# Scaling the probability rows before the turn, one norm chain for two latents, and a step less for the last heads

## The chip, the cores and the metric

The kernel runs on one core of one Trainium2 chip. The metric is the time of one execution on the device, in microseconds (us); lower is better. The engines are named as the profile names them: PE (TensorE, the matrix engine; PEld is its weight load), DVE (VectorE), ACT (ScalarE), POOL (GpSimd) and SP (SyncE, which here only issues transfers). PSUM is the memory that PE writes to, SBUF the working memory; a PSUM bank holds 128 x 512 values of float32.

## The reference, cut to what matters

The program computes two blocks over 256 tokens of width 1024. The first (a mixer and a mixture of experts) is not touched by the change. The second has two layers; each is a mixer, a norm, a convolved feed-forward part and a gate. The first layer's mixer (`mixer_ab`) holds two attentions with eight heads each, the second's (`mixer_c`) a differential attention:

```python
def mixer_ab(x, ...):
    h = x @ w_in
    qa, ka = rope(h[..., :o1]), rope(h[..., o1:o2]); va = h[..., o2:o3]
    out_a = dilated_mixture(qa, ka, va)              # 8 heads of 64
    cq = rms_norm_2(h[..., o3:o4], q_norm, RMS_EPS)  # latent of 384
    ckv = rms_norm_2(h[..., o4:o5], kv_norm, RMS_EPS)  # latent of 256
    qb, kv = cq @ w_q_up, ckv @ w_kv_up
    ...
    out_b = dense_attention(qb, kb, vb, (B_NOPE + B_ROPE) ** -0.5)  # softmax(q k) v, 8 heads
    return concatenate([out_a, out_b]) @ w_out

def mixer_c(x, ...):
    a = softmax(q k / 8)                             # two maps a head, 8 heads
    o = (a[:, :, 0] - lam * a[:, :, 1]) @ v
    return (rms_norm_2(o, subln, LN_EPS) * (1.0 - lambda_init)) @ w_out
```

The dilated mixture of three windows is computed by the kernel as one softmax over all 256 keys, with the logarithm of how often a key is counted added to the scores.

## The kernel before, in words

Everything is in SBUF as 128 partitions by columns; 256 tokens are two halves m = 0, 1. Large matmuls run in three passes with operands split into a high and a low part: ACT copies the high part (`xH`, `w`, `abH`), DVE subtracts it from the source for the low part (`split`, line 463). Weights stream in order: `stream` loads them ahead and splits some pieces ahead of their use (`w<-raw` on ACT, `w<-raw,w` on DVE), each time that `take` asks for the next piece.

The order on every engine is that of the program; nothing is reordered later, and each engine takes its instructions in order. Inside the program, two attentions are written as generators, and a planner (`Side`, line 383) decides where their steps are placed between the projections' matmuls. `Clocked` (line 341) keeps an estimated clock for PE, ACT and DVE: each instruction adds a cost from its columns (DVE: 0.07 us + columns / 960; PE with plain float32: columns / 600) and 0.13 us where it reads what another instruction wrote, that of its own engine too unless both are PE's. A step is due when the last ACT or DVE result of the step before is ready, plus 0.15. After each block of projection matmuls, `side.tick` asks whether the estimated PE clock has reached the due time of the next step, and if so writes the step there, one at most. Of two neighbouring jobs, the one with the earlier due time goes first. `side.finish` writes the remaining steps of a job one after another. All instructions of these engines are recorded under one line (L379), so groups are told apart by tiles.

In `mixer_ab` the latents (`lat`, 672 columns: 384, 256 and 32) come from projection `ab_c`. For each of two latents ACT squares and sums both halves (`j`, `ss`), and DVE runs a chain: one instruction for the mean, ten for the inverse root (`rsqrt`, line 471: a start and three Newton steps of three), and two that scale `lat`. Then the rotation of the last 32 columns, and projection `ab_a` (`tokens(0)`), whose weight halves DVE splits in the same queue.

`pair_attention` (line 1969) serves both attentions with two heads a pair, four pairs p: `turn_head` of the pair before, `score_pair`, `soft` (row maximum on DVE, exponential `pe` with row sum `sm` on ACT), `weigh` of the pair two back (matmuls with the values, then `split` to `abH`, `abL`), a yield, and `diagonal` for both heads; another yield. `diagonal` puts the inverse row sums on a diagonal: two products of the identity, 128 x 128 each. `turn_head` multiplies `pe` by that diagonal, four matmuls a head, which turns the probabilities (keys to the partitions) and scales them at once, and ACT copies the bank to `pp`. `attention_a` is the dilated one (tiles `qkT`, `lnc`, `va`), `attention_b` the one over latents (`bT`, `vb`).

In `mixer_c`, `attention(n, src)` handles two heads, n = 0 to 3: turn q and k; a yield; scores and `soft` of both maps; a yield; the inverse sums, lam, and four DVE products that combine the two maps in `pe`; a yield; `turn_head` without a diagonal, by transposes; a yield; the weighted sum (`oc`), its norm on DVE; a yield; the turn to `ycH` (ACT) and `ycL` (DVE). The output projection `c_out` (`lin_sq`, line 1453) takes its four quarters in order. Quarter 0 is four blocks of six matmuls; quarters 1 to 3 have two blocks each for the first token half, then the second half follows. Quarter 3 reads the result of n = 3.

Of the kernel before, what the change touches and what calls it, by code (L numbers as in the profile page):

```python
# [13 lines left out]
OP = mybir.AluOpType  # L14
# [405 lines left out]
def program(ctx, tc, A, out, dump=None):  # L420
# [11 lines left out]
    def T(shape, name, dt=F32, tag=None):  # L432
        n = 4
        for s in shape[1:]:
            n *= s
        if tag is None:
            for t, lim in (("us", 128), ("uh", 512), ("u1", 1024), ("u2", 2048), ("u4", 4096), ("u8", 8192)):
                if n <= lim:
                    tag = t
                    break  # L440
        uid[0] += 1
        t = sb.tile(list(shape), dt, tag=tag, bufs=BUFS.get(tag, 1), name=f"{name}{uid[0]}")
        return t
# [1485 lines left out]
        for m in range(2):  # L1929
            S.activation(e[:, m], p2[:, m], AF.Exp, bias=nb[:, m:m + 1], scale=scale, accum_out=sm[:, m:m + 1])  # L1930

    def diagonal(r):

        n = r.shape[1]
        d = T([128, n, 128], "diag", tag="u1")
        V.reciprocal(r, r)
        for m in range(n):
            V.tensor_scalar(d[:, m], ident, r[:, m:m + 1], None, op0=OP.mult)
        return d

    def score_pair(get, p, add=None):

# [11 lines left out]
                add(ps)  # L1954
        return banks

    def turn_head(t, e, d=None):

        ps = PS()
        for m in range(2):  # L1960
            for k in range(2):
                o, i = ps[:, (k * 2 + m) * 128:(k * 2 + m) * 128 + 128], e[:, m, k * 128:k * 128 + 128]
                if d is None:
                    P.transpose(o, i, ident)
                else:
                    P.matmul(o, i, d[:, m], start=True, stop=True)
        S.activation(t, ps.rearrange("p (k t) -> p k t", k=2), AF.Copy)

    def pair_attention(get, scale, add, v, y, base, ready=lambda: True):

        probs, pts = {}, {}
        yH, yL = y

        def weigh(p):

            ps, pt = PS(), pts.pop(p)
            for k in range(2):
                for a in range(2):
                    c = slice(p * 128 + a * 64, p * 128 + a * 64 + 64)
                    P.matmul(ps[a * 64:a * 64 + 64, :256], v[:, k, c], pt[:, a, k], start=k == 0, stop=k == 1)  # L1980
            split(yH[:, base + p], yL[:, base + p], ps[:, :256])

        for p in range(6):
            while p > 1 and not ready():
                yield 0.5
            if 0 < p < 5:
                pts[p - 1] = T([128, 2, 2, 256], "pp")
                for a in range(2):
                    turn_head(pts[p - 1][:, a], *probs.pop(2 * p - 2 + a))
            if p < 4:  # L1990
                banks = score_pair(get, p, add)
            if p < 4:
                new = []
                for ps in banks:
                    e, s = T([128, 2, 256], "pe"), T([128, 2, 2], "sm")
                    soft(ps, scale, e, s[:, 0], s[:, 1])
                    new.append((e, s[:, 1]))
            if p > 1:
                weigh(p - 2)
            if p < 4:  # L2000
                yield
                for a, (e, sm) in enumerate(new):
                    probs[2 * p + a] = e, diagonal(sm)
            yield

    def ple_proj(i, p):
# [13 lines left out]
    def mixer_ab(x, evac):  # L2020
# [20 lines left out]
            lin_tok("ab_c", 2 * n, 2, xs, range(2), 336, lambda m, ps: S.activation(lat[:, m, n * 336:n * 336 + 336], ps[:, :336], AF.Copy),  # L2041
                    hold=0 if n else 4, ready=None if n else ready)
        dump("x2", x)
        for c0, w, g in ((0, 384, "ab_q_g"), (384, 256, "ab_kv_g")):
            ss = T([128, 2], "ss3")
            for m in range(2):
                j = T([128, 384], "j3")
                S.activation(j[:, :w], lat[:, m, c0:c0 + w], AF.Square, accum_out=ss[:, m:m + 1])
            V.tensor_scalar(ss, ss, 1 / w, 1e-6, op0=OP.mult, op1=OP.add)
            r = rsqrt(ss, 2)  # L2050
            for m in range(2):
                V.scalar_tensor_tensor(lat[:, m, c0:c0 + w], lat[:, m, c0:c0 + w], r[:, m:m + 1], Rc(g), op0=OP.mult, op1=OP.mult)
        for m in range(2):
            rope2(lat[:, m, 640:].unsqueeze(1), "b", m, 1)
        qk = [T([128, 2, 512], "qa"), T([128, 2, 512], "ka")]
# [87 lines left out]
    def mixer_c(x, evac):  # L2143
        xf = T2([128, 8, 256], "x")
        xs = xs_of(xf)
        yH, yL = T2([128, 8, 256], "yc")

        there = {}

        def attention(n, src):  # L2150


            def get(j):
                h, q = j // 2, slice((j % 2) * 64, (j % 2) * 64 + 64)
                return qk[0][q, h], qk[1][q, h], qk[0][q, 2 + h], qk[1][q, 2 + h]

            qk = to_feat(src, 4)
            yield
            nb, sm = (lambda t: (t[:, 0], t[:, 1]))(T([128, 2, 2, 2, 2], "sm"))
            banks = [ps for h in range(2) for ps in score_pair(get, h)]  # L2160
            es = (lambda t: (t[:, 0], t[:, 1]))(T([128, 2, 2, 2, 256], "pe"))
            for j, ps in enumerate(banks):
                a, h = j % 2, j // 2
                soft(ps, 0.125, es[h][:, a], nb[:, a, h], sm[:, a, h])
            yield
            V.reciprocal(sm[:, 1], sm[:, 1])
            V.scalar_tensor_tensor(sm[:, 1], sm[:, 1], lam, sm[:, 0], op0=OP.mult, op1=OP.mult)
            for h, e in enumerate(es):
                for m in range(2):
                    V.scalar_tensor_tensor(e[:, 0, m], e[:, 1, m], sm[:, 1, h, m:m + 1], e[:, 0, m], op0=OP.mult, op1=OP.add)  # L2170
            sq = T([128, 2, 2], "s2")
            V.scalar_tensor_tensor(sq, sm[:, 0], 1e-5, sm[:, 0], op0=OP.mult, op1=OP.mult)
            yield
            pts = T([128, 2, 2, 256], "pp")
            for h, e in enumerate(es):
                turn_head(pts[:, h], e[:, 0])
            yield
            while n not in there:
                yield 0.5
            ps, vc = PS("oc"), there.pop(n)  # L2180
            for h in range(2):
                for m in range(2):
                    c = slice((2 * m + h) * 128, (2 * m + h) * 128 + 128)
                    for k in range(2):
                        P.matmul(ps[:, c], pts[:, h, k, m * 128:m * 128 + 128], vc[:, k, h * 128:h * 128 + 128], start=k == 0, stop=k == 1)
            o, o2 = (T([128, 4, 128], w) for w in ("oc", "oc2"))
            S.activation(o.rearrange("p h d -> p (h d)"), ps, AF.Copy)
            S.activation(o2.rearrange("p h d -> p (h d)"), ps, AF.Square)
            v = T([128, 4], "cv")
            V.tensor_reduce(v, o2, axis=AX, op=OP.add)  # L2190
            v2 = v.rearrange("p (m h) -> p m h", m=2)
            V.scalar_tensor_tensor(v2, v2, 1 / 128, sq.rearrange("p h m -> p m h"), op0=OP.mult, op1=OP.add)
            r = rsqrt(v, 4)
            V.tensor_tensor(o, o, r.unsqueeze(2).to_broadcast([128, 4, 128]), op=OP.mult)
            yield
            ps = PS()
            for h in range(2):
                for m in range(2):
                    P.transpose(ps[:, h * 256 + m * 128:h * 256 + m * 128 + 128], o[:, 2 * m + h], ident)
            k, p2 = slice(2 * n, 2 * n + 2), ps.rearrange("p (a t) -> p a t", a=2)  # L2200
            S.activation(yH[:, k], p2, AF.Copy, scale=sg)
            V.scalar_tensor_tensor(yL[:, k], p2, sg, yH[:, k], op0=OP.mult, op1=OP.subtract)

        jobs = []

        def ready(m):
            feat_tile(xf, x, m, 8)

        for w, n in C_ORDER:
            if w:  # L2210
                vc = T([128, 2, 256], "vc")
                lin_tok("c_v", n, 1, xs, range(2), 256, lambda m, ps: S.activation(vc[:, m], ps[:, :256], AF.Copy))
                there[n] = vc
                if n == 1:
                    load_p(1)
                continue
            qk = T([128, 2, 512], "qk")
            lin_tok("c_qk", 2 * n, 2, xs, range(2), 512, lambda m, ps: S.activation(qk[:, m], ps, AF.Copy),
                    hold=0 if n else 4, ready=None if n else ready)
            for m in range(2):  # L2220
                rope2(qk[:, m].rearrange("p (h d) -> p h d", d=64)[:, :, :16], "a", m, 8)
            if n > 1:
                side.finish(jobs[n - 2])
            jobs.append(side.add(attention(n, qk), jobs[-1] if jobs else None))
        split_p()
        lin_sq("c_out", xs_of((yH, yL)), evac, {q: lambda q=q: side.finish(jobs[q]) for q in range(4)})
        dump("ycH", yH)
# [136 lines left out]
```

## Time and profile before

| What | us |
|---|---|
| Median of 3 runs | 1422.9 |
| Lowest and highest run | 1419.89, 1423.99 |
| The profiled execution | 1417.77 |
| Its span, first to last instruction | 1416.0 |
| PE busy in it | 1365.2 |
| DVE busy | 836.7 |
| ACT busy | 635.8 |

Times in the profile count from the first instruction of the span. A busy time is the sum over an engine's instructions; the ends of matmuls are modelled, since they are pipelined, so the distance between starts says more than the length of one. The first mixer takes some 700 to 842 us, the second some 1080 to 1180 us. [...]

### The profile page before, as it was taken

Reading aid. Unit: us, or ns where it says so; the run is one execution under the profiler, and the core shown is the slowest. Engines: PE = TensorE matmul, PEld = TensorE weight load, DVE = VectorE, ACT = ScalarE, POOL = GpSimd, SP = SyncE. Lnnn points to the kernel's source line nnn. Section 1 sums busy time; section 2 is a strip of 40 time slices with the busy share of each in tenths; the row PEclk is TensorE's granted clock in tenths of the full one; section 3 lists DMA queues with packets and bytes.
Section 4 is the critical chain, followed back from the end, with each engine's and each line's share of the span. In section 5 each row is a group of like instructions: output and inputs, shape, how many; then the busy total and the mean of one; then the engine's idle time right before and its main releaser. Section 6 shows DMA issues by size and latency. Waiting matters only on the chain.

```text
span 1416.0 us, 20480 instructions
## 1 busy us (share of the span) xinstructions
PE 1365.2 (96%) x8334; PEld 1064.8 (75%) x8334; DVE 836.7 (59%) x1517; ACT 635.8 (45%) x1021; POOL 8.3 (1%) x15
## 2 busy tenths in 40 slices
PE   5999999999999899999999899999999998999998
PEld 2678899878797444343488679999978887999996
DVE  4777457445866511211475586666676888566675
ACT  4643465534433311111356555445536664455541
POOL 0000000000000000000000000000000000000000
PEclk9999999999999999999999999999999999999999
DMA  9523334635469799999742345655544354555630
GB/s 370 223 71 119 149 150 153 250 125 190 175 212 360 301 421 421 421 421 421 283 179 90 120 149 181 207 179 208 175 156 146 127 179 139 188 179 180 216 140 30
DMA packets 44482, 297.42 MB, mean 210 GB/s; under 512 B 5171, under 2 KB 6371, under 8 KB 10017
## 3 DMA queue, kind: packets, MB, share of 16 engines
q1 hardware_dynamic: 41868, 291.02, 54.6%
q10 hardware_dynamic: 1924, 3.27, 0.7%
q0 software_dynamic: 592, 1.79, 0.5%
q8 instruction: 67, 1.10, 0.3%
q14 instruction: 31, 0.25, 0.0%
HBM read 295.00 MB, written 1.05 MB: 209 GB/s over the span
## 4 chain that ended last, share of the span: by engine, by line
PE 58%; DVE 5%; ACT 2%; issue 1%; DVEq 0%; ACTq 0%
PE ps L379 48%; PE pd L379 7%; DVE w L379 1%; PE pa L379 1%; PE pq L379 1%; ACT pe L379 1%; DVE v L379 1%; PE oc L379 1%; DVE sm L379 1%; DVE rs L379 0%; ACT w L379 0%; DVE xL L379 0%; DVE rsa L379 0%; ACT xH L379 0%; ACT oc L379 0%
## 5 line engine op out<-in xcount | busy, mean ns | idle before, releaser
L379 DVE TENSOR_TENSOR w<-raw,w 128x1024 fp32r<-128x1024 f32 (+3 forms) x301 | 346.5, 1195 | 84.6 <-ACT w L379 83.5
L379 ACT ACTIVATE w<-raw 128x1024 fp32r<-128x1024 f32 (+3 forms) x301 | 293.5, 1033 | 10.8 <-DVE w L379 4.8
L379 PE MATMUL ps<-xH,w 128*128 128x256 f32 x1408 | 256.5, 283 | 0.6 <-ACT xH L379 0.6
L379 PEld LDWEIGHTS ps<-xH,w 128*128 128x128 f32 x1408 | 220.6, 192 | 1.8 <-ACT xH L379 1.1
L379 PE MATMUL ps<-xL,w 128*128 128x256 f32 x704 | 199.4, 283 | 0.7 <-DVE xL L379 0.7
L379 PE MATMUL ps<-w,xH 128*128 128x512 f32 (+2 forms) x544 | 150.3, 362 | 4.0 <-ACT xH L379 2.1
L379 PEld LDWEIGHTS ps<-xL,w 128*128 128x128 f32 x704 | 135.0, 192 | 1.8 <-DVE xL L379 1.1
L379 PE MATMUL pd<-w,fh 128*128 128x512 f32 x528 | 125.6, 395 | 0.0
L379 PE MATMUL ps<-raw,xg 128*64 128x512 f32 x512 | 120.0, 600 | 0.0
L379 PE MATMUL ps<-hH,w 128*128 128x256 f32 (+1 forms) x608 | 115.7, 287 | 0.0
L379 PEld LDWEIGHTS pd<-w,fh 128*128 128x128 f32 x528 | 98.2, 189 | 21.6
L379 PEld LDWEIGHTS ps<-w,xH 128*128 128x128 f32 x544 | 95.4, 189 | 19.3 <-ACT xH L379 4.0
L379 PEld LDWEIGHTS ps<-hH,w 128*128 128x128 f32 (+1 forms) x608 | 94.9, 187 | 7.9 <-issue 2.7
L379 PE MATMUL ps<-w,xL 128*128 128x512 f32 (+2 forms) x272 | 97.8, 360 | 1.9 <-DVE xL L379 1.7
L379 PE MATMUL ps<-w,hH 128*128 128x512 f32 (+1 forms) x288 | 88.1, 390 | 0.0
L379 PE MATMUL ps<-hL,w 128*128 128x256 f32 (+1 forms) x304 | 85.9, 283 | 0.0
L379 PEld LDWEIGHTS ps<-raw,xg 128*64 128x64 f32 x512 | 33.3, 137 | 55.7 <-issue 51.9
L379 DVE SCALAR_TENSOR_TENSOR fc<-ps,par,fc 128x255 f32<-128x255 f32 x88 | 42.4, 482 | 51.5 <-ACT fc L379 49.9
L379 ACT ACTIVATE fc<-ps,par 128x256 f32<-128x256 f32 x44 | 24.8, 564 | 92.3 <-PE ps L379 66.4
L379 PEld LDWEIGHTS ps<-w,hH 128*128 128x128 f32 x288 | 52.2, 188 | 13.8 <-issue 2.7
L379 PEld LDWEIGHTS ps<-w,xL 128*128 128x128 f32 x272 | 51.3, 189 | 11.9 <-DVE xL L379 5.1
L379 PE MATMUL ps<-raw,hid 128*64 128x512 f32 x256 | 57.4, 593 | 0.0
(445 smaller groups left out, 1858.7 us busy)
## 6 DMA issues: line engine op xcount, KB each, us to landing
raw<-in_moe_gu SPq DMA_DIRECT2D x63, 1024.0 KB, 14.1
raw<-in_moe_down SPq DMA_DIRECT2D x32, 1024.0 KB, 12.8
raw<-in_mod SPq DMA_DIRECT2D x24, 1024.0 KB, 5.0
raw<-in_ffn_gate SPq DMA_DIRECT2D x22, 1024.0 KB, 4.8
raw<-in_ffn_up SPq DMA_DIRECT2D x22, 1024.0 KB, 4.9
raw<-in_ffn_down SPq DMA_DIRECT2D x22, 1024.0 KB, 4.8
raw<-in_w_brg SPq DMA_DIRECT2D x12, 1024.0 KB, 5.9
raw<-in_ple_gate SPq DMA_DIRECT2D x8, 1024.0 KB, 4.8
```

Source lines behind the costliest of these rows:

```text
L379: return f(*args, **kw)
```

## The change

Four edits. (1) In `mixer_ab`, `diagonal` is replaced by `scaled`: DVE multiplies the probability rows by the inverse row sums in place, and `turn_head` turns them by transposes in both mixers. (2) `weigh` no longer calls `split`: both parts are written by DVE, the high part by a copy, the low part by the subtraction. (3) The two latents' sums go into one tile, and one `rsqrt` over four columns serves both. (4) In `mixer_c`, the yield between `soft` and the combination of the two maps falls away for n = 3.

```diff
-    def diagonal(r):
-
-        n = r.shape[1]
-        d = T([128, n, 128], "diag", tag="u1")
+    def scaled(e, r):
+
         V.reciprocal(r, r)
-        for m in range(n):
-            V.tensor_scalar(d[:, m], ident, r[:, m:m + 1], None, op0=OP.mult)
-        return d
+        for m in range(2):
+            V.tensor_scalar(e[:, m], e[:, m], r[:, m:m + 1], None, op0=OP.mult)
+        return e
...
-    def turn_head(t, e, d=None):
+    def turn_head(t, e):
 
         ps = PS()
         for m in range(2):
             for k in range(2):
-                o, i = ps[:, (k * 2 + m) * 128:(k * 2 + m) * 128 + 128], e[:, m, k * 128:k * 128 + 128]
-                if d is None:
-                    P.transpose(o, i, ident)
-                else:
-                    P.matmul(o, i, d[:, m], start=True, stop=True)
+                P.transpose(ps[:, (k * 2 + m) * 128:(k * 2 + m) * 128 + 128], e[:, m, k * 128:k * 128 + 128], ident)
...
-            split(yH[:, base + p], yL[:, base + p], ps[:, :256])
+            V.tensor_copy(yH[:, base + p], ps[:, :256])
+            V.tensor_tensor(yL[:, base + p], ps[:, :256], yH[:, base + p], op=OP.subtract)
...
-                    turn_head(pts[p - 1][:, a], *probs.pop(2 * p - 2 + a))
+                    turn_head(pts[p - 1][:, a], probs.pop(2 * p - 2 + a))
...
-                    probs[2 * p + a] = e, diagonal(sm)
+                    probs[2 * p + a] = scaled(e, sm)
...
-        for c0, w, g in ((0, 384, "ab_q_g"), (384, 256, "ab_kv_g")):
-            ss = T([128, 2], "ss3")
+        latents = ((0, 384, "ab_q_g"), (384, 256, "ab_kv_g"))
+        ss = T([128, 2, 2], "ss3")
+        for i, (c0, w, _) in enumerate(latents):
             for m in range(2):
                 j = T([128, 384], "j3")
-                S.activation(j[:, :w], lat[:, m, c0:c0 + w], AF.Square, accum_out=ss[:, m:m + 1])
-            V.tensor_scalar(ss, ss, 1 / w, 1e-6, op0=OP.mult, op1=OP.add)
-            r = rsqrt(ss, 2)
+                S.activation(j[:, :w], lat[:, m, c0:c0 + w], AF.Square, accum_out=ss[:, i, m:m + 1])
+            V.tensor_scalar(ss[:, i], ss[:, i], 1 / w, 1e-6, op0=OP.mult, op1=OP.add)
+        r = rsqrt(ss.rearrange("p i m -> p (i m)"), 4)
+        for i, (c0, w, g) in enumerate(latents):
             for m in range(2):
-                V.scalar_tensor_tensor(lat[:, m, c0:c0 + w], lat[:, m, c0:c0 + w], r[:, m:m + 1], Rc(g), op0=OP.mult, op1=OP.mult)
+                V.scalar_tensor_tensor(lat[:, m, c0:c0 + w], lat[:, m, c0:c0 + w], r[:, 2 * i + m:2 * i + m + 1], Rc(g), op0=OP.mult, op1=OP.mult)
...
-            yield
+            if n < 3:
+                yield
             V.reciprocal(sm[:, 1], sm[:, 1])
```

## Rows read from the trace of the kernel before

**Rows 1.** The page, busy time of each engine, share of the span, instructions.
```profile
PE 1365.2 (96%) x8334; PEld 1064.8 (75%) x8334; DVE 836.7 (59%) x1517; ACT 635.8 (45%) x1021; POOL 8.3 (1%) x15
```
**Rows 2.** Windows: length, busy time (instructions) by engine, granted clock, DMA share, GB/s.
```profile
785.00:812.00 27.00, 22.45 (x160) 16.51 (x159) 12.62 (x44) 14.83 (x47) 0.00 (x0) 1.00 0.20 71
812.00:842.00 30.00, 30.00 (x150) 24.11 (x151) 25.74 (x48) 14.38 (x24) 0.00 (x0) 1.00 0.36 122
...
1162.00:1166.00 4.00, 3.95 (x15) 3.03 (x15) 3.05 (x6) 3.47 (x5) 0.00 (x0) 0.61 0.57 238
...
1176.00:1180.00 4.00, 3.35 (x8) 2.68 (x9) 2.93 (x4) 1.06 (x1) 0.00 (x0) 0.57 0.00 0
```
**Rows 3.** Groups by form, 735 to 830 us: busy us, mean ns, idle before.
```profile
L379 PE MATMUL ps<-diag,pe 128*128 128x128 f32 x128 | 15.9, 278 | 4.6 <-DVE diag L379 4.6
...
L379 DVE TENSOR_SCALAR diag<-c_base,sm 128x128 f32<-128x128 f32 x32 | 7.7, 284 | 0.6
...
L379 DVE TENSOR_TENSOR abL<-ps,abH 128x256 fp32r<-128x256 f32 x8 | 3.3, 423 | 8.3 <-ACT abH L379 8.3
```
**Rows 4.** Time line of PE, 784 to 813 us: start, length, work, idle before it.
```profile
784.26 1.95 PE L379 MATMUL ps<-diag,pe 128*128 128x128 f32 x16
...
790.18 2.02 PE L379 MATMUL ps<-diag,pe 128*128 128x128 f32 x16 [1.79 <-DVE diag L379]
...
802.90 2.02 PE L379 MATMUL ps<-diag,pe 128*128 128x128 f32 x16 [2.76 <-DVE diag L379]
...
811.92 0.73 PE L379 MATMUL ps<-w,abH 128*128 128x512 f32 x2
```
**Rows 5.** Time line of DVE, 787 to 806 us.
```profile
798.69 0.69 DVE L379 TENSOR_REDUCE sm<-ps 128x2 f32<-128x512 f32 x1 [1.49 <-PE ps L379]
...
801.93 0.42 DVE L379 TENSOR_TENSOR abL<-ps,abH 128x256 fp32r<-128x256 f32 x1 [1.56 <-ACT abH L379]
```
**Rows 6.** Time line of DVE, 718 to 729 us.
```profile
721.95 0.17 DVE L379 TENSOR_SCALAR rs<-ss 128x2 int32<-128x2 int32 x1
...
723.91 0.88 DVE L379 SCALAR_TENSOR_TENSOR lat<-lat,rs,row_b 128x256 f32<-128x256 f32 x2
```
**Rows 7.** Time line of DVE, 1150 to 1178 us.
```profile
1156.67 1.23 DVE L379 TENSOR_TENSOR w<-raw,w 128x1024 fp32r<-128x1024 f32 x1 [2.46 <-ACT w L379]
...
1160.40 0.17 DVE L379 RECIPROCAL sm<-sm 128x4 f32<-128x4 f32 x1
...
1160.87 1.67 DVE L379 SCALAR_TENSOR_TENSOR pe<-pe,sm 128x256 f32<-128x256 f32 x4
...
1168.94 0.69 DVE L379 TENSOR_REDUCE cv<-oc 128x4 f32<-128x512 f32 x1 [0.75 <-ACT oc L379]
...
1172.44 3.49 DVE L379 TENSOR_TENSOR w<-raw,w 128x1024 fp32r<-128x1024 f32 x3
1175.85 0.74 DVE L379 SCALAR_TENSOR_TENSOR ycL<-ps,lam,ycH 128x512 fp32r<-128x512 f32 x1
```
**Rows 8.** Time line of PE, 1139 to 1141 us.
```profile
1139.72 1.04 PE L379 MATMUL ps<-c_base,pe 128*128 128x128 f32 x8
```
**Rows 9.** Groups by form on DVE, the whole span.
```profile
L379 DVE TENSOR_SCALAR e<-e,sm 128x512 f32<-128x512 f32 x16 | 7.8, 487 | 0.6
```
**Rows 10.** Time line of PE, 724 to 729 us.
```profile
727.23 0.50 PE L379 MATMUL ps<-w,xH 128*128 128x512 f32 x1 [1.85 <-DVE w L379]
```
**Rows 11.** Time line of ACT in the stretch from 716 us.
```profile
718.29 0.19 ACT L379 ACTIVATION_READ_ACCUMULATOR j<-lat 128x1 f32 x1
...
719.09 0.19 ACT L379 ACTIVATION_READ_ACCUMULATOR j<-lat 128x1 f32 x1
```
**Rows 12.** Time line of ACT, 1151 to 1164 us.
```profile
1155.45 0.24 ACT L379 ACTIVATION_READ_ACCUMULATOR pe<-ps,sm 128x1 f32 x1
```
**Rows 13.** Time line of PE, 1157 to 1181 us.
```profile
1161.50 1.59 PE L379 MATMUL ps<-c_base,pe 128*128 128x128 f32 x8 [2.80 <-DVE pe L379]
...
1176.65 0.80 PE L379 MATMUL ps<-w,ycL 128*128 128x512 f32 x1 [1.83 <-DVE ycL L379]
```

## Prediction

> **What bounds the kernel now.** The page comes first: PE is busy for 96% of the span and DVE for 59% [rows 1], so a change gains where it takes work from PE or shortens a wait in front of PE. All edits lie in two stretches: the first mixer's (716 to 842 us) and the end of the second's (1150 to 1180 us). [...] Then come the groups by form, to see how often a thing is done [rows 3], and the time lines of PE, DVE and ACT, read backwards from each wait of PE: which DVE instruction ended it, and what stood in front of that one in DVE's queue [rows 4 to 7]. DVE takes its instructions in order, so an instruction that waits holds all that are written after it.
>
> **Turning the heads.** 128 matmul rows carry the diagonals, 16 to a turn of two heads [rows 3]. Two heads are 2 x 2 x 2 = 8 matmuls, so each matmul leaves two rows: it passes through PE twice. The 16 rows take 1.95 us, of which the last row's modelled end is some 0.27, so one starts every (1.95 - 0.27)/15 = 0.112 us and a turn holds PE for 16 x 0.112 = 1.79 us [rows 4]. The second mixer does the same turn with transposes: 8 rows in 1.04 us, one every (1.04 - 0.27)/7 = 0.110 us, one row each [rows 8]; that is 0.88 us. Each of eight turns gets 0.91 us shorter: **7.3 us** of PE.
>
> On DVE each head loses two 128x128 products of 284 ns [rows 3] and gets two of 128x256, which no row shows. The same operation takes 487 ns on 128x512 [rows 9]; on the line through both, 128 more columns cost (487 - 284)/3 = 68 ns, so I take 352 ns, an estimate; the ends are 284 and 487. Two heads thus cost DVE 0.27 us more a turn, 2.2 us over 32. Where a turn comes straight behind its scaling, it now runs at DVE's pace: four scalings and two reciprocals, some 1.5 us from the first, instead of PE's own 0.88.
>
> The copy of the weighted heads' high part goes from ACT to DVE: eight copies of 128x256 out of PSUM. The nearest rows: a product half as wide, 284 ns, and the subtraction of the same width that reads the same PSUM bank, 423 ns [rows 3]. I take the nearer, 423: 3.4 us more for DVE. What it removes is a hand-over: DVE sat idle 1.56 us until ACT's copy came, which stood behind four exponentials on ACT, and only behind that subtraction came the reciprocals for the next turn [rows 5]; this was much of PE's longest wait, 2.76 us [rows 4].
>
> So the waits. Today there are two, 1.79 and 2.76 us, 4.55 together [rows 4]. The planner charges a scaled head 0.07 + 256/960 us a product, and a hand-over between the two since both write one tile, against 0.07 + 128/960 now: 2.0 us for two heads against 1.2. By its rule (the earlier due of two neighbouring jobs goes first) the first score step of the dilated heads now comes ahead of the latent heads' second, and from there the two change places. Worked by hand in that order, with 1.7 us for two row maxima (798.69 to 801.93 - 1.56 [rows 5]), 0.8 for a copy and a subtraction and 1.4 for two scaled heads, PE waits some 0.5 us before one turn and 1.4 before another, and loses 0.6 at DVE's pace in turns: 2.5 to 3.4 in all, against 4.55. I count **1.2 us** of gain. From both sides: without the removed hand-over and with each of six turns at DVE's pace, the waits grow by 4; with a perfect order all 4.55 go. Behind the last turns stand the output projection's matmuls, from 811.92 on [rows 4], in a window where PE has no gap [rows 2], so what is won before it arrives whole. None of the edited steps issues a DMA; the queues of SP and POOL keep their order.
>
> **One norm chain.** PE waits 1.85 us for a weight's low half [rows 10], which stands in DVE's queue behind two norm chains [rows 6]. The second chain's ten short instructions, from 721.95 to 723.91, go: 1.96 us. But the joint chain starts when all four squares are there: the last of them ends 0.80 us after the second, which starts the chain today [rows 11]. That leaves **1.2 us**, all inside the 1.85; ends: 0 and 1.85.
>
> **The last heads of the second mixer.** DVE is through with the maxima at 1156.67 - 2.46 = 1154.21 and idles to 1156.67; ACT's last exponential ends at 1155.69 [rows 7, 12]. The reciprocal starts at 1160.40 only, behind four others, and PE waits 2.80 us for its products [rows 7, 13]. Without the yield the reciprocal stands right behind the maxima: it starts at 1155.8, and with the durations of today (0.47 to the first product, 1.67 for four) the products end at 1157.9. What stands behind it now starts later: the weight half of 1156.67, the low part of the group before, the split of p and another weight half, each by some 1.2 us; the first readers on PE come after 1161, so this costs nothing, and would cost up to 1.2 if they came at once. The turn moves up too: the step is due earlier, and I read the planner's arithmetic as placing it after the first of four blocks of six matmuls instead of after the fourth. PE then waits about 2.4 us there, and has the other three blocks to fill the time in which the weighted sum's norm runs; were it left after the fourth, the products would be ready before PE is, with much the same end. The weighted sum then ends near 1161.5; the norm, 1168.94 to 1172.44 today, starts near 1162.8 and ends at 1166.4; behind it stand the five weight halves that the blocks in between ask for, (1175.85 - 1172.44)/3 = 1.14 us each, then the low part, at 1172.1 to 1172.8 instead of 1175.85 + 0.74 [rows 7]. PE's matmul of 1176.65 [rows 13] moves to 1172.9: **3.8 us**. The clock adds or takes: the windows at 0.61 and 0.57 lose 4 x 0.39 = 1.6 and 4 x 0.43 = 1.7 us [rows 2]. If both slow stretches stay, 2.2 remain, if both go, 5.4; ends: 0 and 6.5.
>
> **Sum.** 7.3 + 1.2 + 1.2 + 3.8 = 13.5 us. The profiled execution took 1417.8 us (span 1416.0, and 1.8 around it) and becomes 1404.3; it lies 5.1 under the median of the runs, 1422.9, so for a median I forecast 1422.9 - 13.5 = **1409.4 us**. About 0.3%, 4.3 us, is what a measurement here can tell from no change.
>
> **Rivals.**
> *The clock falls at the turns.* The two waits of nearly equal length in the trace differ in what follows: 2.76 us and then matmuls, clock 1.00; 2.80 us and then transposes, clock 0.61 [rows 2, 4, 13]. The change puts transposes behind the first mixer's waits. If each of two loses 1.6 us there, and the slow stretches at 1162 and 1176 both stay, the gain is 13.5 - 3.2 - 1.6 = 8.7: 1414.2. Against it: the waits get shorter. [...]
> *DVE sets the pace.* All six turns that are not under projection matmuls end with DVE's scaling: they win 0.3 instead of 0.91, and the waits stay: 2 x 0.91 + 6 x 0.3 + 1.2 + 3.8 = 8.6, 1414.3. For it: DVE's additions, 5.6 us; against: DVE is busy 12.62 of 27 us there [rows 2].
> *Nothing much arrives.* The shorter turns turn into longer waits one for one, since maxima, exponentials and scaling form a ring through all engines; only the norm chain and 2 us at the end remain: 1419.7.
> *Slower.* The scaled rows come late at every turn, each wait as long as today's longest: 8 x 2.76 - 4.55 = 17.5 more, less 7.3, 1.2 and 3.8: 5.2 us slower, 1428.1. The place is DVE's queue before the turns; it decides from a mean wait of (4.55 + 12.3)/8 = 2.1 us a turn. Against: the first turns have projection matmuls before them that cover a wait.
>
> **Chances.** Forecast 0.58 (own range 1404 to 1413), clock 0.12, DVE's pace 0.13, nothing much 0.11, slower 0.06. Range: 1403 to 1417.5, which holds the first three but for a small part of the forecast's own tail; its low end has all bounds of the last heads (6.5), the norm (1.85) and most of the waits. Faster by over 0.3%: 0.58 + 0.12 + 0.13 = 0.83; within: 0.11; slower: 0.06.
>
> **What would show it.** Right: 64 rows in place of 128 for these turns, about 0.11 us apart; DVE products of 128x256 near 350 ns; no DVE idle time for ACT's copy; the first output projection matmul of the first mixer, at 811.92 now, some 9 us earlier, 1.2 of it from the norm chain; the reciprocal of the last heads within 0.3 us of the last exponential. Wrong: waits for the scaled rows over 1.5 us at more than two turns; a granted clock under 1.00 between 785 and 812; the low part of the last group still behind weight halves at 1175.

## The result, and the profile after

The changed kernel takes 1410.61 us (median of 4 runs, 1408.6 to 1410.85), the kernel before in the same session 1422.23: ratio 0.9905, 95% interval 0.9876 to 0.9933. The forecast was 1409.4, range 1403 to 1417.5, faster. The profiled execution went from 1417.77 to 1408.6, its span from 1416.0 to 1406.8: 9.2 us, where the sum said 13.5.

Matmul starts repeat from execution to execution within 0.05 us as long as the clock is the same (the changed kernel and e9, the same kernel, differ by 0.00, 0.02 and 0.03 us in the table's distances), so each part is measured between two landmarks on PE. **A**: from the last expert matmul (`ps<-raw,hid`) to the first transposes of `lat`; it holds the norm chain. **B**: from there to the first layer's projection of `p`; it holds the first mixer's turns. **C**: from the first output-projection product of the second mixer to the first low part in the feed-forward behind it; it holds the last heads.

PE, time line of the changed kernel at B's two ends and at C's end (start, length, work, idle before it), then the same three of the kernel before:

```profile
728.28 1.25 PE L379 MATMUL ps<-c_base,lat 128*128 128x128 f32 x10
...
829.60 5.82 PE L379 MATMUL pq<-w,p 128*128 128x512 f32 x24
...
1188.02 0.38 PE L379 MATMUL ps<-xL,w 128*128 128x256 f32 x1 [0.73 <-DVE xL L379]
```
```profile
729.86 1.25 PE L379 MATMUL ps<-c_base,lat 128*128 128x128 f32 x10
...
838.87 2.33 PE L379 MATMUL pq<-w,p 128*128 128x512 f32 x9
...
1197.26 0.39 PE L379 MATMUL ps<-xL,w 128*128 128x256 f32 x1 [0.34 <-DVE xL L379]
```

The distances of all kernels run (us; the experiments are below):

| Kernel | A | B | C | Median |
|---|---|---|---|---|
| before | 35.74 | 109.01 | 44.20 | 1422.2 to 1423.2 |
| changed | 34.35 | 101.32 | 44.19 | 1410.6 |
| e1 two rows | 34.37 | 107.72 | 44.23 | 1416.3 |
| e2 turns alone | 37.31 | 110.20 | 44.22 | 1421.4 |
| e3 norm alone | 34.39 | 109.04 | 44.13 | 1419.8 |
| e4 last heads alone | 35.73 | 112.15 | 42.91 | 1421.2 |
| e5 ACT copies | 34.35 | 111.19 | 43.96 | 1421.4 |
| e6 other buffer | 34.38 | 101.27 | 42.12 | 1408.4 |
| e7 low part first | 34.38 | 102.84 | 42.52 | 1413.6 |
| e8 copy behind | 34.35 | 99.63 | 40.83 | 1404.5 |
| e9 changed again | 34.35 | 101.30 | 44.22 | 1411.4 |

The medians leave out three executions of over 3400 us, one each of e4, e7 and the kernel before. A of e2 and B of e2, e4, e5 and e7 hold stretches at a lower granted clock (a share of PE's full clock; as means over 4 us down to 0.68 at the end of A of e2, and to 0.57, 0.57, 0.50 and 0.63 in the four B); in the other traces it is 1.00 throughout A and B. In C the clock falls twice, to 0.50 in windows of 1 us of before and changed, with some 1.7 us lost each time, in the traces of before, changed, e1, e5, e6 and e9; once for twice as long in e7 (0.80, 0.50 and 0.84 over 4 us each, 3.4 us lost); once in e4 (0.73 and 0.85, 1.7 us) and not at all in e8 (1.00 behind both waits). In e2 and e3 the mean from 1160 to 1240 us is 0.96, as in the kernel before.

So the change won 1.39 us in A, 7.69 in B and nothing in C; 0.2 lie ahead of A, and behind C the two kernels run alike (213.3 us each to the end of the last matmul).

**The first mixer.** Page of the changed kernel, PE's line (before: [rows 1]); then groups by form, 720 to 835 us (before: [rows 3]):

```profile
PE 1359.7 (97%) x8270; PEld 1056.6 (75%) x8270; DVE 839.6 (60%) x1515; ACT 632.6 (45%) x1013; POOL 8.3 (1%) x15
```
```profile
L379 DVE TENSOR_SCALAR pe<-pe,sm 128x256 f32<-128x256 f32 x32 | 9.9, 351 | 0.6
L379 DVE TENSOR_TENSOR abL<-ps,abH 128x256 fp32r<-128x256 f32 x8 | 3.4, 424 | 0.3
L379 DVE CAST abH<-ps 128x256 fp32r<-128x256 f32 x8 | 3.4, 420 | 1.8 <-PE ps L379 1.8
...
L379 PE MATMUL ps<-c_base,pe 128*128 128x128 f32 x64 | 9.3, 278 | 2.7 <-ACT pe L379 2.3
```

64 rows stand where 128 stood, PE counts 64 instructions less, a scaling takes 351 ns (352 estimated), a copy 420 (423 taken). The subtraction's idle time for ACT's copy, 8.3 us in [rows 3], is 0.3. Time line of PE (before: [rows 4]) and windows (before: [rows 2]; the columns are the same):

```profile
785.19 1.35 PE L379 MATMUL ps<-c_base,pe 128*128 128x128 f32 x8 [0.66 <-ACT pe L379]
786.47 1.13 PE L379 MATMUL ps<-qkT 64*128 64x256 f32 x8
...
789.68 1.09 PE L379 MATMUL ps<-c_base,pe 128*128 128x128 f32 x8
790.61 1.89 PE L379 MATMUL ps<-bT 96*128 96x256 f32 x8
...
795.19 1.36 PE L379 MATMUL ps<-c_base,pe 128*128 128x128 f32 x8 [1.67 <-ACT pe L379]
...
805.63 0.73 PE L379 MATMUL ps<-w,abH 128*128 128x512 f32 x2
```
```profile
785.00:812.00 27.00, 24.84 (x150) 16.09 (x151) 21.42 (x60) 19.73 (x50) 0.00 (x0) 1.00 0.26 86
...
1150.00:1154.00 4.00, 4.00 (x23) 3.54 (x22) 2.24 (x3) 1.07 (x3) 0.00 (x0) 0.74 0.94 295
1166.00:1170.00 4.00, 4.00 (x13) 3.14 (x12) 3.65 (x5) 0.00 (x0) 0.00 (x0) 0.60 0.35 143
```

Two waits remain, 0.66 and 1.67, 2.33 together against 4.55. Four of the eight turns, the two behind these waits among them, go at DVE's pace: from the start to the next work 786.47 - 785.19 = 1.28 us, against 790.61 - 789.68 = 0.93 for one whose rows are ready. The first output projection matmul of the mixer, which the forecast expected some 9 us earlier, went from 811.92 to 805.63, only 6.3: in the kernel before one more turn stood behind it. Where all turns are done the gain is there: the projection of p starts 838.87 - 829.60 = 9.27 us earlier.

**The norm chain.** DVE's joint chain, and PE's wait behind it (before: [rows 6, 10]):

```profile
719.29 0.17 DVE L379 TENSOR_SCALAR rs<-ss 128x4 int32<-128x4 int32 x1
...
721.27 1.94 DVE L379 SCALAR_TENSOR_TENSOR lat<-lat,rs,row_b 128x384 f32<-128x384 f32 x4
```
```profile
725.65 0.50 PE L379 MATMUL ps<-w,xH 128*128 128x512 f32 x1 [0.49 <-DVE w L379]
```

PE's wait of 1.85 is 0.49.

**The last heads.** DVE (before: [rows 7]), then ACT, then PE (before: [rows 13]); to compare with before, add the 9.24 us by which all of this stretch already comes earlier:

```profile
1146.49 0.18 DVE L379 RECIPROCAL sm<-sm 128x4 f32<-128x4 f32 x1 [1.51 <-ACT pe L379]
...
1158.53 5.76 DVE L379 TENSOR_TENSOR w<-raw,w 128x1024 fp32r<-128x1024 f32 x5
1164.21 0.74 DVE L379 SCALAR_TENSOR_TENSOR ycL<-ps,lam,ycH 128x512 fp32r<-128x512 f32 x1
1164.87 3.49 DVE L379 TENSOR_TENSOR w<-raw,w 128x1024 fp32r<-128x1024 f32 x3
1168.27 0.68 DVE L379 SCALAR_TENSOR_TENSOR v<-v,ps 128x512 f32<-128x512 f32 x1
1171.66 1.23 DVE L379 TENSOR_TENSOR w<-raw,w 128x1024 fp32r<-128x1024 f32 x1 [1.98 <-ACT w L379]
1172.81 0.68 DVE L379 SCALAR_TENSOR_TENSOR v<-v,ps 128x512 f32<-128x512 f32 x1
```
```profile
1170.57 1.06 ACT L379 ACTIVATE w<-raw 128x1024 fp32r<-128x1024 f32 x1 [7.21 <-PE ps L379]
```
```profile
1147.60 1.79 PE L379 MATMUL ps<-c_base,pe 128*128 128x128 f32 x8 [2.22 <-DVE pe L379]
...
1165.01 0.50 PE L379 MATMUL ps<-w,ycL 128*128 128x512 f32 x1 [1.96 <-DVE ycL L379]
...
1178.35 1.29 PE L379 MATMUL ps<-c_base,v 128*128 128x128 f32 x8 [1.00 <-DVE v L379]
```

The reciprocal stands right behind the last exponential, and the product that reads the last group's low part comes at 1165.01, with 9.24 added 1174.25, instead of 1176.65: 2.40 us earlier. But behind it DVE splits four weight halves, and the last of them, at 1171.66, stands between the two column halves of the layer norm (`v`). It waits 1.98 us for ACT, and ACT's copy waits for PE until 1170.57. So the layer norm is late, PE waits 1.00 us for it where it had no wait before, and at C's end all 2.40 us are gone.

### The profile page after: what moved, and what is told of

The parts are those of the page before. It is cut to its first block, busy times and chain, and to the rows that moved or that the text cites. A ratio compares the mean times of both kernels' runs of the same rounds, so it can differ in the third digit from the quotient of the medians.

```text
span 1406.8 us, 20329 instructions
## 1 busy us (share of the span) xinstructions
PE 1359.7 (97%) x8270; PEld 1056.6 (75%) x8270; DVE 839.6 (60%) x1515; ACT 632.6 (45%) x1013; POOL 8.3 (1%) x15
## 3 DMA queue, kind: packets, MB, share of 16 engines
q0 software_dynamic: 592, 1.79, 0.5%
## 4 chain that ended last, share of the span: by engine, by line
PE 56%; DVE 6%; ACT 2%; issue 1%; ACTq 0%; DVEq 0%
PE ps L379 47%; PE pd L379 8%; DVE w L379 2%; PE pa L379 1%; DVE v L379 1%; ACT pe L379 1%; DVE rs L379 1%; PE oc L379 1%; DVE xL L379 0%; DVE sm L379 0%; PE pq L379 0%; ACT w L379 0%; DVE bs L379 0%; DVE rsa L379 0%; ACT xH L379 0%
## 6 DMA issues: line engine op xcount, KB each, us to landing
raw<-in_moe_down SPq DMA_DIRECT2D x32, 1024.0 KB, 13.5
```

## The experiments

**e1: the rows on PE.** In the first mixer a product with the identity in place of the transposes.

```diff
-                P.transpose(o, i, ident)
+                P.matmul(o, i, ident, start=True, stop=True)
```

> The changed kernel with one thing put back: in the first mixer the scaled rows are turned by a plain float32 product with the identity in place of transposes; DVE's work and the order stay. If what counts is how many rows PE runs (16 against 8 a turn), 64 rows of 0.11 us come back, 7 us, less what the turns at DVE's pace hide (1.3 us now against 1.79): 5 to 7 us slower than the changed kernel, about 1416; the distance from the first latent transposes to the second layer part's first projection of p (101.3 us in the changed kernel, 109.1 in the one before) becomes 106 to 108. If the gain came from DVE's shorter hand-over and the new order of steps, less than 2 us comes back, 103 at most.

B was 107.72, 6.40 us more than in the changed kernel; median 1416.27, ratio to before 0.9929 (0.9908 to 0.9951). PE waited 0.66, 1.67 and 0.68 us: the same two waits and one more. The rows count nearly in full; 0.9 of 7.3 us had been hidden by DVE's pace in four turns, which get 0.67 us longer here where the others get 0.91 to 0.96.

**e2: the turns alone.** The kernel before with `scaled` and the transposes; `split` (ACT's copy), two norm chains and the yield stay.

> The kernel before with the scaled rows and the transposes alone: ACT still copies the high part of the weighted heads, two norm chains, the yield stays. The theory (rows and order) expects nearly all of the first mixer's gain: the distance from the latent transposes to p's projection 101.3 to 102.5 us, 109.1 before; whole time about 7 us under the kernel before, 1415. The rival that the removed wait for ACT's copy carries much of it expects 104 or more.

B was 110.20, median 1421.41, ratio 0.9979 (0.9958 to 1.0000). PE of e2, then the changed kernel's turn behind the one at 795.19:

```profile
792.65 1.36 PE L379 MATMUL ps<-c_base,pe 128*128 128x128 f32 x8 [2.84 <-ACT bT L379]
...
798.67 1.09 PE L379 MATMUL ps<-c_base,pe 128*128 128x128 f32 x8
...
805.38 1.94 PE L379 MATMUL ps<-c_base,pe 128*128 128x128 f32 x8 [2.87 <-DVE pe L379]
...
812.32 1.09 PE L379 MATMUL ps<-c_base,pe 128*128 128x128 f32 x8
```
```profile
799.69 1.09 PE L379 MATMUL ps<-c_base,pe 128*128 128x128 f32 x8
```

Part of B is the clock, which fell in or behind both waits (0.79 and 0.78 over 4 us each from 792, 0.57 and 0.58 from 804); against the changed kernel these two stretches, from turn to next turn, are (798.67 - 792.65) - (799.69 - 795.19) = 1.52 and (812.32 - 805.38) - 4.50 = 2.44 us longer. At full clock B would be 110.20 - 1.52 - 2.44 = 106.2: the rival was right, and the turns alone bring only 2.8 of 7.7 us. Of the 4.9 that are missing, 3.4 are the two longer waits and 1.4 lie behind the mixer, where PE waits 0.93 us for the layer norm.

**e5: ACT copies again.** The changed kernel with `split` in `weigh`; nothing else differs, not even the order of the steps.

```diff
-            V.tensor_copy(yH[:, base + p], ps[:, :256])
-            V.tensor_tensor(yL[:, base + p], ps[:, :256], yH[:, base + p], op=OP.subtract)
+            split(yH[:, base + p], yL[:, base + p], ps[:, :256])
```

> The changed kernel with ACT copying the high part of the weighted heads again; the order of the steps stays as in the changed kernel, joint norm chain and last heads too. Theory: the hand-over to ACT is what makes PE wait before the turns; the two waits of 0.66 and 1.67 us become about 2.85 each, 3.4 us more, and after waits of this length the granted clock falls in part of the executions, so that its runs spread over granted clocks of 0.986 to 0.993: median 1414.5 to 1418, the distance from latent transposes to p's projection 104.5 at full clock, more where the clock fell. The rival that rows on PE alone carry the gain (DVE's copy is worth nothing): 101.3 to 102, median 1410 to 1412, clock 0.993 in all runs.

B was 111.19, median 1421.42 (12 runs), ratio 0.9991 (0.9973 to 1.0009): in the medians, without the two copies on DVE the whole change is worth nothing. DVE's subtraction of e5, PE's turns and two windows behind them:

```profile
792.52 0.42 DVE L379 TENSOR_TENSOR abL<-ps,abH 128x256 fp32r<-128x256 f32 x1 [2.54 <-ACT abH L379]
792.87 0.15 DVE L379 RECIPROCAL sm<-sm 128x2 f32<-128x2 f32 x1
```
```profile
793.55 1.94 PE L379 MATMUL ps<-c_base,pe 128*128 128x128 f32 x8 [2.84 <-ACT bT L379]
...
800.60 1.09 PE L379 MATMUL ps<-c_base,pe 128*128 128x128 f32 x8
...
807.30 1.94 PE L379 MATMUL ps<-c_base,pe 128*128 128x128 f32 x8 [2.87 <-DVE pe L379]
```
```profile
796.00:800.00 4.00, 4.00 (x16) 2.28 (x14) 1.27 (x3) 0.45 (x2) 0.00 (x0) 0.53 0.00 0
...
808.00:812.00 4.00, 4.00 (x16) 2.75 (x15) 1.52 (x7) 1.19 (x2) 0.00 (x0) 0.50 0.00 0
```

ACT's copy stands behind four exponentials, the subtraction behind the copy, the reciprocal behind the subtraction. B's 9.87 us over the changed kernel are, from turn to turn: 2.19 and 1.20 of longer waits, 2.55 and 2.49 where the clock is at half behind these waits, and 1.4 behind the mixer, where PE waits 0.93 us for the layer norm. The two waits came as expected. At full clock B would be 111.19 - 2.55 - 2.49 = 106.15, not 104.5, mostly for what lies behind the mixer, and the median of 1421.42 lies above the expected 1414.5 to 1418. Why the layer norm is late in e2 and e5 was not followed up.

**e3: the norm chain alone**, on the kernel before.

> The kernel before with the joint norm chain alone. The theory expects PE's wait of 1.85 us for the weight's low part to become 0.5 and everything after it to come 1.2 to 1.6 us earlier, to the end: about 1421, which cannot be told from 1422.2 by the times alone; the place where the shift is read is the first latent transposes and the mixer's end. A rival: the first mixer's ring of steps takes the 1.4 us back, so that the projection of p comes less than 0.5 us earlier.

A was 34.39, B 109.04: 1.35 us earlier, and all of it kept to the end. The rival fell.

**e4: the last heads alone**, the yield left out of the kernel before.

> The kernel before with the last heads' yield left out alone. In the changed kernel the first product with the last group's low part came 2.4 us earlier and the first low part of the feed-forward not at all: DVE's layer norm of the first token half stands behind a weight half whose buffer PE still reads. This theory expects the same here: about 2.4 us at the one place, 0 (within 0.3) at the other, total 1422, no change. A rival, that the gain was lost only beside the other edits or to the clock, expects 1.5 to 3.8 us left at the feed-forward: 1419 to 1420.

C was 42.91, 1.29 less than before and neither forecast. DVE's late half is there just as in the changed kernel:

```profile
1184.31 1.23 DVE L379 TENSOR_TENSOR w<-raw,w 128x1024 fp32r<-128x1024 f32 x1 [1.97 <-ACT w L379]
```
```profile
1164.00:1168.00 4.00, 3.99 (x26) 3.26 (x26) 2.50 (x4) 2.35 (x5) 0.00 (x0) 1.00 0.99 297
```

Up to the product with the last group's low part the step brings 3.68 us here (19.90 us from the first output-projection product, 23.58 before), where the changed kernel had 2.40; 1.29 of it are left at C's end. What differs from the changed kernel is the clock behind the turn: 1.00 here in the windows 1160 to 1168, 0.93 and 0.74 in the changed kernel's 1140 to 1150 and 1150 to 1154, which lose up to 10 x 0.07 + 4 x 0.26 = 1.7 us. The kernel before and the changed one, with two falls each in C, both take 44.2: there the step brings nothing. That the 1.29 is the fall that is missing here is argued, not shown; e6 and e8, with two falls and none, differ by 1.29 too. The same execution shows the unedited first mixer with the clock fallen, so that B is 112.15: the turn by matmuls behind the wait of 1.79 us takes 3.44 us, where it takes 2.02 in [rows 4].

```profile
791.76 3.44 PE L379 MATMUL ps<-diag,pe 128*128 128x128 f32 x16 [1.79 <-DVE diag L379]
```
```profile
792.00:796.00 4.00, 4.00 (x20) 3.86 (x20) 1.51 (x8) 1.68 (x5) 0.00 (x0) 0.57 0.00 0
```

**e6: another buffer for one weight half.** Tiles of this size share 19 buffers, and a new tile gets one whose last reader is already written. The step that moved changes which these are: in the changed kernel as built the weight half in question gets the buffer of an output-projection half that the second token half still needs, in the kernel before it got one that DVE had read last. One buffer taken ahead of it moves it on to one of that kind.

```diff
+                if name == "ffn_up1" and i == order.index(("ffn_up1", 0, 8, 256, "c")) and u == 0:
+                    G.memset(T([128, 2048], "spare")[:, :1], 0.0)
                 halves[i, u] = T2(list(w.shape), "w")
```

> The changed kernel with one more buffer taken, and never used, ahead of one weight half (the first of the feed-forward's second matrix), so that this half gets a buffer that DVE has already freed; nothing else differs. Theory (that half waits for a buffer that PE still reads, and the layer norm of the first token half stands behind it on DVE): DVE's wait of 1.98 us for this half goes, PE's wait of 1.00 before the turn of the norm's result and of 0.34 and 0.73 behind it go or shrink, and the first low part of the feed-forward comes 1.3 to 1.9 us earlier: from the first product of the output projection to it 42.3 to 42.9 us where the changed kernel takes 44.2, if the clock falls at the same places. Rival (the tail is bound by DVE's sum of work or by the clock): less than 0.4 us.

C was 42.12, 2.07 us less than the changed kernel and a little more than expected, at the same falls of the clock (0.73 and 0.59 in the windows 1150 to 1154 and 1166 to 1170); median 1408.37, ratio to before 0.9900 (0.9880 to 0.9919). The half no longer waits, nor does PE for the layer norm:

```profile
1169.61 1.21 DVE L379 TENSOR_TENSOR w<-raw,w 128x1024 fp32r<-128x1024 f32 x1
```
```profile
1165.02 0.50 PE L379 MATMUL ps<-w,ycL 128*128 128x512 f32 x1 [1.95 <-DVE ycL L379]
1177.19 1.03 PE L379 MATMUL ps<-c_base,v 128*128 128x128 f32 x8
```

**e7: the low part ahead of two weight halves.** As e6 with two buffers, and `c_out and b > 0` becomes `c_out and b > 1` in the rule of how many pieces are split ahead.

> As the run before with two such buffers, and two weight halves that stood in front of the last group's low part on DVE are written behind it (fewer pieces are split ahead in the output projection's second quarter). PE's wait of 1.96 us for that low part should go (it comes 2.3 us earlier). If DVE's sum of work behind it bounds the stretch, the feed-forward's first low part gains no more than 0.3 us over the run before; if the waits themselves do, up to 1.9 us more, and another 1.7 where the slow clock stretch behind the wait goes too: 40.4 to 42.0 us for the same distance.

PE's wait for the low part is gone, but it waits 2.73 us for the layer norm instead, and the clock falls at that wait; C 42.52, no gain over e6, as expected if DVE's sum of work bounds the stretch. From 1164 to 1192 us DVE is busy 3.79 to 4.00 of every 4 us. It is not the only bound: in e8 C is 40.83 with the same work, where the clock does not fall (1.00 in the windows behind both waits).

```profile
1183.18 1.94 PE L379 MATMUL ps<-c_base,v 128*128 128x128 f32 x8 [2.73 <-DVE v L379]
```
```profile
1184.00:1188.00 4.00, 4.00 (x14) 3.32 (x13) 3.79 (x11) 1.48 (x3) 0.00 (x0) 0.50 0.52 217
```

**e8: the copy behind the scaling.** As e6, and `weigh` returns its two DVE instructions, which run after `scaled`.

```diff
-            if p > 1:
-                weigh(p - 2)
+            out = weigh(p - 2) if p > 1 else None
             if p < 4:
                 yield
                 for a, (e, sm) in enumerate(new):
                     probs[2 * p + a] = scaled(e, sm)
+            if out:
+                out()
```

> As the run with the other buffer, and in the first mixer the two DVE instructions that write the high and low part of the weighted heads (0.42 us each) are written behind the scaling of the pair's rows instead of before the yield. In the changed kernel they stand in front of the reciprocal for the next turn (the two start 0.79 us before it) and PE waits 0.66 and 1.67 us for these turns. If that place in DVE's queue is what PE waits for, the waits become about 0 and 0.9, and the distance from the latent transposes to p's projection 99.8 to 100.4 us (101.3 in the changed kernel): 1406.5 to 1408 in all. If the exponentials or the banks of PSUM, which are now held longer, set the turns, it stays at 101 or more.

B was 99.63, C 40.83 (with no fall of the clock there), median 1404.52, ratio to before 0.9872 (0.9848 to 0.9896): it beats both kernels, the changed one by 6.9 us in the same session (e9). The profiled executions of the two lie 5.2 apart, 1.7 in B and 3.4 in C; of C, 2.1 is the other buffer (e6), and the rest comes where the clock does not fall. The waits of 0.66 and 1.67 are gone, as expected; two of 0.85 and 0.84 stand before turns that had none, and the order of PE's work at the mixer's end differs too, so that B holds more than the one move:

```profile
791.52 1.35 PE L379 MATMUL ps<-c_base,pe 128*128 128x128 f32 x8 [0.85 <-DVE pe L379]
...
800.68 1.35 PE L379 MATMUL ps<-c_base,pe 128*128 128x128 f32 x8 [0.84 <-DVE pe L379]
```

**e9: the changed kernel again.**

> The changed kernel once more, with more runs, beside runs of the kernel before on the same chip, for the granted clock. In four runs it was 0.993 each time, with waits of at most 1.67 us before the turns; the kernels with waits of 2.8 us there lie between 0.984 and 0.993. If the length of the wait decides whether the clock falls, at least two thirds of its runs stay at 0.992 or more, median 1409 to 1412, ratio 0.990 to 0.993; if it is chance of the execution, its runs spread as those of the kernel before (about half under 0.991) and the difference of the medians falls to 9 to 10 us.

Median 1411.37, ratio 0.9926 (0.9898 to 0.9953). Three of six runs had a granted clock of 0.993, three 0.989 or 0.990: neither two thirds nor the spread of before, of whose 54 runs beside the experiments six had 0.993 or more. With the first four runs it is seven of ten.

## Why the prediction was right, and where it was not

**The total was right partly by luck.** The traces show 9.2 us, not 13.5. The median fell by 11.6 (e9: 11.4), and what it fell by beyond 9.2 goes with the clock, to which most executions of the kernel before lose more (48 of its 54 beside the experiments are at 0.983 to 0.992). At a granted clock of 0.993 or more before takes 1418.9 (mean of six runs), changed 1410.0 (of seven): 8.9 apart. The forecast set its sum, made from one execution at 0.994, against a median in which most executions have a lower clock; so a gain of this kind, shorter waits and fewer falls, was in no term.

**Turning the heads, 7.3, and the waits, 1.2.** Together 8.5 forecast, 7.69 measured, and the order of the steps was as worked out. The split was wrong. The rows are worth 6.40 (e1), since four of eight turns go at DVE's pace. And the two terms do not add: the turns without DVE's copies bring 2.8 (e2), the copies on top 4.8 (e5, at full clock), the rows on top of the copies 6.4. The step that failed is the one that sized the removed hand-over as part of 1.2 us of waits: without it the waits are 2.84 and 2.87 us, 4.9 us of B are lost, and in the medians of e2 and e5 next to nothing arrives, as in the rival "nothing much arrives". Its cause was named (the copy behind four exponentials). Its weight stood only in an end of the term: waits that grow by 4 without it would have left 3.3 of the 8.5, near the 2.8 of e2, but that end was reckoned with six turns at DVE's pace besides, where the runs show four.

**One norm chain, 1.2.** 1.39 in the changed kernel, 1.35 alone; right in mechanism and size.

**The last heads, 3.8.** Nothing arrived. The term up to the low part was right: with both slow stretches it said 2.2, and 2.40 came; with one of them gone 3.8, and 3.68 came in e4, where the one behind the turn is missing. The step that failed is the one that ended at the matmul of 1176.65, as if what is won there stayed. Behind it DVE was the next to be late: four weight halves and the layer norm of the first token half, one half in a buffer that PE still read. e6 shows it: the buffer alone gives 2.07 back. The forecast looked for the next wait on PE up to that matmul, not on DVE behind it, and not at what moving a step does to the buffers.

**The clock.** "The clock falls at the turns" did not come to pass: 1.00 from 785 to 812. The kind of turn alone does not decide here: the clock fell at turns by plain matmuls (e4: 0.57 and 0.72 over 4 us) and stayed at 1.00 through transposes behind waits of 0.66 and 1.67 us. What the runs show is that falls go with long waits. In the first mixer, in eleven traces, none of the waits before a turn of under 1 us had a fall in or behind it; of the fifteen from 1.67 to 2.87 us seven had one.

That shorter waits are the cause of fewer falls is argued, not shown. It fits e1, e8 and e5 (granted clock 0.993 to 0.996 in all of e1's six runs, 0.995 or more in five of e8's six, 0.984 to 0.992 in eleven of e5's twelve), though this figure is that of the whole execution, with falls outside the mixer too. But e7, with the changed kernel's first mixer, had a fall behind 1.67 us (0.63 over 4 us), so it is a matter of chance too. And a part of the rival stays open: of the waits of 1.79 us and more, all four in front of transposes had a fall (e2, e5: 2.84 and 2.87), of the six in front of plain matmuls two (before, e3, e4: 1.79 to 2.77); and e1, with plain matmuls behind waits as long as the changed kernel's, kept 0.993 or more in six of six runs, the changed kernel in seven of ten. No run puts both kinds behind the same wait of over 2 us.

## What to carry to other kernels

Where steps run in a ring through three engines, much of the work taken from one can turn into its wait unless the next hand-over in the ring gets shorter as well (here 4.9 of 7.7 us): look for the instruction that stands in front of the releaser on the releaser's engine. A step moved ahead is won only at the point from which nothing waits for anything else (here 2.40 us at the last group's low part, nothing at C's end): follow it past the first reader, on the queue of the engine that feeds it, and see which buffer each later load or split will get once the step has moved. Compare medians with medians and traces with traces, and look at the granted clock of both before a sum from one is set against the other.

## What the hardware showed that was not expected

The same instructions with nearly the same waits ran at different clocks. Behind PE's waits of 2.23 and 1.95 us in the second mixer the granted clock fell to 0.73 and 0.59 in e6, as means over 4 us (in the changed kernel, with 0.74 and 0.60 there, windows of 1 us show 0.50), and stayed at 1.00 in e8, behind waits of 2.21 and 1.98 us. A fall at a turn of the first mixer cost 1.5 to 2.6 us (e2, e4, e5, e7), one in C some 1.7, in e7 3.4. So a wait of some 2 us cost its own length and, in part of the traces, another 1.5 us or more. What decides in which execution the clock falls was not shown.
